# Sums of gated products in the up-projection: half products and sums on VectorE with accumulating DMAs, in place of sums on GpSimd

## The chip, the cores and the metric

The kernel runs on one core of a Trainium2 chip. The metric is the device time of one execution in microseconds (us). The core has five engines that work side by side, each through its own instructions in order: TensorE (PE, matmuls; PEld is its weight load), VectorE (DVE), ScalarE (ACT), GpSimd (POOL) and SyncE (SP, which here only issues DMAs). They meet through semaphores. DMAs move data between DRAM and the on-chip memory; the kernel issues them from SP's queue, from ScalarE's and, after the change, from GpSimd's.

## The reference

One layer of a causal encoder on `x` of shape [1, 2048, 1024]: a gated linear attention mixer, and then a feed-forward block with a causal depthwise convolution. The change lies in the second:

```python
def conv_ffn(h, w_up, conv_w, conv_b, w_down):
    u = causal_dwconv(h @ w_up, conv_w, conv_b)      # h: 2048 x 1024, u: 2048 x 5632
    g, val = jnp.split(u, 2, axis=-1)
    return (jax.nn.silu(g) * val) @ w_down           # (2048 x 2816) @ (2816 x 1024)
```

`causal_dwconv` adds, for each channel, three neighbouring tokens with a weight each and a bias. All is float32.

## The kernel before

The large matrix products are done by Strassen's method in Winograd's form: both operands are cut in 2 x 2 blocks, and seven products `p1` to `p7` of sums of blocks replace eight. float32 accuracy comes from splitting each operand into a high and a low part (`split`, L188 a cast on ScalarE, L189 a subtraction on VectorE) and multiplying three times (`mm3p`, L179 to L181).

The program runs in stages. The mixer takes the first 873 us or so. Then comes the up-projection (`phase_u`), in two halves of 1024 tokens (`s` = 0 and 1; 877 to 1357 us and 1357 to 1750 us of the profile), and then the down-projection (to the end).

In the up-projection the 22 blocks of 128 features are taken in pairs, `f` = 2g and 2g + 1, 11 groups in each half. For a group, the order of jobs is p1, p5, p6, p7, p4, p2, p3, each for the even and then the odd feature, 12 matmuls of 128x512 per job. `ua` and `uc` are PSUM banks that several products add to; what must be kept of `ua` on the way is copied out by ScalarE as `c` (L1237 after p1 and p6; L1333 after p7) before the next product adds to it. The finished columns `u` (both the gate's and the value's) go through the convolution (`conv`: L1253 ACT, L1255 twice DVE, L1257 ACT for silu) into `t`, 128 features by 1024 tokens.

`gated(s, f)`, called at the end of p3, multiplies gate and value (L1262). What the down-projection needs are the seven sums of blocks of that product. With a11 and a21 the two halves of the even feature's tokens and a12 and a22 those of the odd feature's, they are p1 = a11, p2 = a12, p4 = a22, p5 = a21 + a22, p6 = p5 - a11, p3 = a12 - p6 and p7 = a11 - a21. `tiles2` gives the two halves of a tile, each four blocks of 128. The first three are stored as they are (SP's DMAs, L1266, L1269, L1270), the other four are made on GpSimd (L1276, L1280, L1278, L1280) in tiles with the tag `as` and stored by SP (L1282), all to `ad[s, o, q]` in DRAM.

The tag `as` has six buffers (`AB`). They are shared: the copies `c` of L1333 use them, and, in the first half only, the operands `h2p` that are prepared for the second half (`spread` over `prep_h2`: ScalarE casts the high part, VectorE subtracts for the low part, ScalarE issues the two DMAs to `hd`, L841). A tile can only be filled when the last reader of that buffer is done, DMAs among them. The second half then reads `hd` through SP (L904, `h_p`).

The weights of a group are loaded two jobs and seven jobs into the group before it (`load`, L1204, tiles `ur`, by SP). Sums of weights (`us`, L1214 to L1232) are made on GpSimd.

Functions given to `later_do(us, fn)` are issued when a modelled clock, which `adv` moves by each matmul's modelled time, has gone that far. Within each engine the order of instructions is then set by a scheduler when the program is built, so an edit can move instructions that it doesn't name.

In the down-projection `use` adds the seven products to the output (`xe`, `xd` for two blocks of tokens, `acc` for partial sums, `pb` for the bank). `load_step` (L1388) reads `ad` as `da`, L1464 loads the residual `xs` from `x1d`.

Of the kernel before, what the change touches and what calls it, by code (L numbers as in the profile page):

```python
# [10 lines left out]
F32 = mybir.dt.float32  # L11
# [3 lines left out]
ALU = mybir.AluOpType  # L15

P = 128
# [8 lines left out]
def hybrid_kernel(  # L26
# [17 lines left out]
    nc = tc.nc  # L44
    x = x[0]
# [19 lines left out]
    AB = 6  # L65
# [26 lines left out]
    DLEAD = 4  # L92
    DLOAD = 6
    DWLOAD = 3

    cst = ctx.enter_context(tc.tile_pool(name="cst", bufs=1))
    gx = ExitStack()
# [12 lines left out]
    pools = {}  # L110

    def scratch(shape, name):
        return dr.tile(shape, F32, tag=name, name=name)
# [10 lines left out]
    ad = {(s, o, q): scratch([P, 512], f"ad_{s}_{o}_{q}") for s in range(NS) for o in OPS for q in range(NQ)}  # L124

    def mm_ps(name):
        return ps.tile([P, 512], F32, tag="mm", name=name, bufs=4)
# [23 lines left out]
    def later_do(us, fn):  # L151
        heapq.heappush(delayed, (clock["now"] + us, next(seq), fn))
# [1029 lines left out]
    def tiles2(ap):  # L1182

        v = ap.rearrange("p (j c k) -> p c j k", c=2, k=P)
        return v[:, 0], v[:, 1]

    def tiles1(ap):
        return ap.rearrange("p (j k) -> p j k", k=P)
# [3 lines left out]
    def phase_u():  # L1192
        raws, wops, sums, made = {}, {}, {}, {}
# [46 lines left out]
        def new_u(s, i, f):  # L1240
            c = f + i * NF
            u = pools["us"].tile([P, TS + 2], F32, tag="u", name=f"u_{s}_{c}", bufs=3)
            nc.gpsimd.tensor_copy(u[:, 0:2], halo[:, c, :])
            made["u", i, f] = u
            return tiles2(u[:, 2:2 + TS])
# [13 lines left out]

        def gated(s, f):  # L1260
            t, v = made.pop(("t", 0, f)), made.pop(("t", 1, f))
            nc.vector.tensor_mul(t, t, v)  # L1262
            made["a", f % 2] = tiles2(t)
            q = f // 2
            if f % 2 == 0:
                nc.sync.dma_start(tiles1(ad[s, "p1", q]), made["a", 0][0])  # L1266
                return
            (a11, a21), (a12, a22) = made["a", 0], made["a", 1]
            nc.sync.dma_start(tiles1(ad[s, "p2", q]), a12)  # L1269
            nc.sync.dma_start(tiles1(ad[s, "p4", q]), a22)  # L1270
            last = None
            for o, fn, x, y in (("p5", "add", a21, a22), ("p6", "sub", None, a11), ("p3", "rsub", None, a12), ("p7", "sub", a11, a21)):
                t = pools["us"].tile([P, 512], F32, tag="as", name=f"as_{s}_{q}_{o}", bufs=AB)
                tv = tiles1(t)
                if fn == "add":
                    nc.gpsimd.tensor_add(tv, x, y)  # L1276
                elif fn == "rsub":
                    nc.gpsimd.tensor_sub(tv, y, last)  # L1278
                else:
                    nc.gpsimd.tensor_sub(tv, last if x is None else x, y)  # L1280
                last = tv
                nc.sync.dma_start(ad[s, o, q], t)  # L1282

        load(0, 0)
        load(0, 1)
# [3 lines left out]
        for k, (s, g, o, f) in enumerate(jobs):  # L1289
# [23 lines left out]
            if o == "p1":  # L1313
                a = bank["a", f] = mm_ps(f"ua_{s}_{f}")
# [5 lines left out]
            elif o == "p6":  # L1320
                a = bank["a", f]
                mm3p(a, pairs, first=False, more=True)
                made["u2", f] = copied(f"c2_{s}_{f}", a)
            elif o == "p2":
                pb = mm_ps(f"ub_{s}_{f}")
                mm3p(pb, pairs)
                ev, _ = new_u(s, 0, f)
                nc.vector.tensor_add(ev, tiles1(pb), tiles1(made.pop(("p1", f))))  # L1328
            elif o == "p7":
                a = bank["a", f]  # L1330
                mm3p(a, pairs, first=False, more=True)
                u3 = pools["us"].tile([P, 512], F32, tag="as", name=f"c3_{s}_{f}", bufs=AB)
                nc.scalar.copy(u3, a)  # L1333
                ev, od = new_u(s, 1, f)
                made["ev", f] = ev
                nc.vector.tensor_add(od, tiles1(bank["c", f]), tiles1(u3))
            elif o == "p4":
                a = bank.pop(("a", f))
                mm3p(a, pairs, first=False, more=True)
                nc.scalar.copy(made.pop(("ev", f)), tiles1(a))  # L1340
                conv(s, 1, f)
            else:
                c = bank.pop(("c", f))
                mm3p(c, pairs, first=False, more=True)
                _, od = tiles2(made["u", 0, f][:, 2:2 + TS])
                nc.vector.tensor_add(od, tiles1(c), tiles1(made.pop(("u2", f))))
                conv(s, 0, f)
                gated(s, f)
# [4 lines left out]
    araw, wraw, aops, wops, chain, xs, acc, wgrp = {}, {}, {}, {}, {}, {}, {}, {}  # L1353
# [20 lines left out]
    def load_wr(k):  # L1374
        o, s, q = steps[k]
        if s == 0:
            wraw[o, q] = []
            for ij in blocks_of(o):
                r = next(dstep["wr"])
                nc.sync.dma_start(r, block(q, *ij))  # L1380
                wraw[o, q].append(r)
# [35 lines left out]
    def d_load(n):  # L1417
        while dstep["wloaded"] < min(len(steps), n - DLOAD + DWLOAD):
            load_wr(dstep["wloaded"])
            dstep["wloaded"] += 1  # L1420
        while dstep["loaded"] < min(len(steps), n):
            load_step(dstep["loaded"])
            dstep["loaded"] += 1
# [42 lines left out]
    def final_tile(t, nw):  # L1466
        n = 2 if t + 2 == S // P else 1
        sls = [slice(i * D // n, (i + 1) * D // n) for i in range(n)]
        x = xs[t]
        junk = acc[t // TT, t % TT // 2].bitcast(BF16)  # L1470
        ssq = small("ssq", f"ssqf_{t}", 2, "f")
        for i, sl in enumerate(sls):
            nc.scalar.activation(junk[:, sl], x[:, sl], AF.Square, accum_out=ssq[:, i:i + 1])
        var = small("var", f"varf_{t}", 1, "f")
        if n == 2:
            nc.vector.tensor_add(ssq[:, 0:1], ssq[:, 0:1], ssq[:, 1:2])
        nc.vector.tensor_scalar(var, ssq[:, 0:1], 1.0 / D, EPS, op0=ALU.mult, op1=ALU.add)
        rstd = small("rstd", f"rstdf_{t}", 1, "f")
        nc.gpsimd.tensor_tensor(rstd, var, neghalf, op=ALU.pow)
        for sl in sls:  # L1480
            nc.vector.scalar_tensor_tensor(x[:, sl], x[:, sl], rstd, nw[:, sl], op0=ALU.mult, op1=ALU.mult)
            nc.scalar.dma_start(out[t * P:(t + 1) * P, sl], x[:, sl])

    def use(o, s, m, pb, nw):

        e, d = s * TT + 2 * m, s * TT + 2 * m + 1
        c1, c2 = slice(0, 512), slice(512, 1024)
        xe, xd = xs[e], xs[d]
        add = nc.vector.tensor_add
        if o == "p1":  # L1490
            acc[s, m] = dx.tile([P, 512], F32, tag=f"acc{s}_{m}", name=f"acc_{s}_{m}")
            nc.scalar.copy(acc[s, m], pb)
            add(xe[:, c1], xe[:, c1], pb)
        elif o == "p5":
            add(xd[:, c2], xd[:, c2], pb)
            add(xe[:, c2], xe[:, c2], pb)
        elif o == "p6":
            add(acc[s, m], acc[s, m], pb)
            nc.gpsimd.tensor_add(xe[:, c2], xe[:, c2], acc[s, m])
        elif o == "p7":  # L1500
            add(acc[s, m], acc[s, m], pb)
            nc.gpsimd.tensor_add(xd[:, c1], xd[:, c1], acc[s, m])
            nc.gpsimd.tensor_add(xd[:, c2], xd[:, c2], acc[s, m])
        elif o == "p2":
            add(xe[:, c1], xe[:, c1], pb)
        elif o == "p4":
            add(xd[:, c1], xd[:, c1], pb)
            final_tile(d, nw)
        else:
            add(xe[:, c2], xe[:, c2], pb)  # L1510
            final_tile(e, nw)

    nwf = dx.tile([P, D], F32, tag="nwf", name="nwf")
    more = [dx.tile([P, 512], F32, tag=f"wr{i}", name=f"dwr_{i}") for i in range(2 * (DWLOAD + 1) - len(dstep["wr"]))]
    dstep["wr"] = itertools.cycle(dstep["wr"] + more)
    for n, (o, s) in enumerate(units):
        banks = [(mm_ps if n % 2 == 0 else aux_ps)(f"pd_{o}_{s}_{m}") for m in range(PAIRS)]
        last = n + 1 == len(units)
# [53 lines left out]
```

## Time and profile before

| | |
|---|---|
| three runs | 2180.76, 2174.13, 2181.27 us; median 2180.76 |
| profiled execution | span 2176.4 us from the first to the last instruction; its own device time isn't listed apart from the three runs |
| instructions | 28914 |
| mean granted TensorE clock | 0.986 |
| TensorE's longest waits outside the change's stages | 11.7 us for `x` (L383) at the start, 6.1 us for `og` (L728) in five places |
| DMA traffic | 411.76 MB, mean 189 GB/s |
| DMA queues | hardware queues only: q1 48.2%, q10 8.6% of 16 engines' span |

Each row of a view of the profile reads: start and duration in us, engine, line of the kernel, operation, `out<-in` by the program's names, shapes, and in brackets the idle time before it and what ended it. A name ending in `_p` stands for several tiles of a kind. `SPq` and `ACTq` are the issuing of DMAs on SP and ScalarE. In grouped rows, busy time and mean ns of one stand behind the count, then the idle time before them with its most frequent cause.

### The profile page before, as it was taken

To read this page: it belongs to the slowest core of one execution; us is meant where nothing else is said; L and a number is where in the kernel's file an instruction comes from. 1 tells how busy PE (TensorE), PEld (TensorE's weight loads), DVE (VectorE), ACT (ScalarE), POOL (GpSimd) and SP (SyncE) were. 2 spreads that over 40 slices of the span, in tenths; PEclk is the share of its full clock that TensorE was granted. 3 is DMA by queue.
4 is the path that set the end of the run, shared out by engine and by line. 5 is a ranking of instruction groups with operands and counts; after the bars stand their busy time and mean duration, and the time that the engine had idled before them with its cause. 6 is when DMAs were issued, how large, how long until landed. Compare 5 with 4: busy or idle time off the path is not lost.

```text
span 2176.4 us, 28914 instructions
## 1 busy us (share of the span) xinstructions
PE 2086.0 (96%) x9832; PEld 1730.6 (80%) x9832; DVE 1648.3 (76%) x2168; ACT 1104.3 (51%) x2024; POOL 734.9 (34%) x606
## 2 busy tenths in 40 slices
PE   7999999989998999799999998999999999999998
PEld 5788788878887887677888777888888877888886
DVE  8756888798888663778899776988888776457564
ACT  5555756665565775444554453554445533333342
POOL 2000011111111002456666554666565444037010
PEclk9999999999999999999999999999999999999999
DMA  6646684578557999654453458242424567254453
GB/s 219 223 165 211 213 297 137 159 229 298 178 195 251 323 344 365 207 163 131 146 184 102 146 177 291 88 131 76 139 77 124 187 247 269 97 184 160 141 182 113
DMA packets 305124, 411.76 MB, mean 189 GB/s; under 512 B 23742, under 2 KB 160110, under 8 KB 304976
## 3 DMA queue, kind: packets, MB, share of 16 engines
q1 hardware_dynamic: 267440, 346.99, 48.2%
q10 hardware_dynamic: 37536, 62.93, 8.6%
q8 instruction: 77, 1.26, 0.2%
q14 instruction: 71, 0.58, 0.1%
HBM read 266.70 MB, written 143.13 MB: 188 GB/s over the span
## 4 chain that ended last, share of the span: by engine, by line
PE 65%; DVE 13%; DMA 10%; issue 6%; ACT 2%; POOL 2%; SPq 0%; ACTq 0%; DVEq 0%; POOLq 0%
PE pd_p L180 5%; PE pd_p L181 5%; PE pd_p L179 5%; PE ua L179 5%; PE ua L180 5%; PE ua L181 5%; DVE t L1255 4%; DMA h_p<-hd_p 2%; PE uc L179 2%; PE uc L181 2%; PE uc L180 2%; PE mp_Y L180 2%; PE mp_Y L181 2%; PE mp_Y L179 2%; PE mp_R L179 2%
## 5 line engine op out<-in xcount | busy, mean ns | idle before, releaser
L179 PE MATMUL ua<-h_p,uw_p 128*128 128x512 f32 x704 | 279.0, 396 | 28.0 <-ACT c L1237 23.2
L1255 DVE SCALAR_TENSOR_TENSOR t<-u,cw,t 128x1024 f32<-128x1024 f32 x176 | 270.4, 1542 | 10.3 <-ACT t L1253 9.1
L180 PE MATMUL ua<-h_p,uw_p 128*128 128x512 f32 x704 | 277.7, 394 | 0.0
L181 PE MATMUL ua<-h_p,uw_p 128*128 128x512 f32 x704 | 277.2, 394 | 0.0
L180 PE MATMUL pd_p<-dw_p,da 128*128 128x512 f32 x616 | 240.7, 391 | 3.4 <-DVE da L189 3.4
L181 PE MATMUL pd_p<-dw_p,da 128*128 128x512 f32 x616 | 240.3, 390 | 0.0
L179 PE MATMUL pd_p<-dw_p,da 128*128 128x512 f32 x616 | 240.1, 390 | 0.0
L189 DVE TENSOR_TENSOR da<-da_p,da 128x512 fp32r<-128x512 f32 x154 | 131.4, 906 | 105.4 <-ACT da L188 105.3
L189 DVE TENSOR_TENSOR uw_p<-ur,uw_p 128x512 fp32r<-128x512 f32 x176 | 168.6, 979 | 48.8 <-ACT uw_p L188 48.4
L188 ACT CAST da<-da_p 128x512 fp32r<-128x512 f32 x154 | 85.3, 619 | 207.9 <-PE pd_p L181 149.9
L179 PEld LDWEIGHTS ua<-h_p,uw_p 128*128 128x128 f32 x704 | 134.4, 191 | 59.6 <-ACT c L1237 31.8
L188 ACT CAST uw_p<-us 128x512 fp32r<-128x512 f32 x132 | 82.1, 622 | 169.0 <-POOL us L1217 130.7
L189 DVE TENSOR_TENSOR uw_p<-us,uw_p 128x512 fp32r<-128x512 f32 x132 | 127.9, 978 | 47.8 <-ACT uw_p L188 46.8
L181 PEld LDWEIGHTS ua<-h_p,uw_p 128*128 128x128 f32 x704 | 134.5, 191 | 28.6
L180 PEld LDWEIGHTS ua<-h_p,uw_p 128*128 128x128 f32 x704 | 134.5, 191 | 27.9
L180 PEld LDWEIGHTS pd_p<-dw_p,da 128*128 128x128 f32 x616 | 116.0, 188 | 28.7 <-DVE da L189 4.7
L179 PE MATMUL uc<-h_p,uw_p 128*128 128x512 f32 x352 | 137.2, 390 | 0.9 <-DVE u L1328 0.9
L679 POOL TENSOR_TENSOR r<-r,gnw 128x512 f32<-128x512 f32 x32 | 46.9, 1466 | 268.6 <-ACT r L678 228.2
L181 PE MATMUL uc<-h_p,uw_p 128*128 128x512 f32 x352 | 136.9, 389 | 0.0
L180 PE MATMUL uc<-h_p,uw_p 128*128 128x512 f32 x352 | 136.9, 389 | 0.0
L181 PEld LDWEIGHTS pd_p<-dw_p,da 128*128 128x128 f32 x616 | 116.1, 188 | 24.1
L179 PEld LDWEIGHTS pd_p<-dw_p,da 128*128 128x128 f32 x616 | 116.1, 188 | 24.0
(278 smaller groups left out, 5474.8 us busy)
## 6 DMA issues: line engine op xcount, KB each, us to landing
ur<-in_ffn_w_up_dram SPq DMA_DIRECT2D x168, 256.0 KB, 3.7
da_p<-ad_p SPq DMA_DIRECT2D x154, 256.0 KB, 3.8
h_p<-hd_p SPq DMA_DIRECT2D x56, 512.0 KB, 8.0
ad_p<-as_p SPq DMA_DIRECT2D x88, 256.0 KB, 2.3
ad_p<-t SPq DMA_DIRECT2D x66, 256.0 KB, 3.1
x<-in_x_dram SPq DMA_DIRECT2D x32, 512.0 KB, 4.7
ch<-in_ffn_w_down_dram SPq DMA_DIRECT2D x61, 256.0 KB, 4.2
hr_A_p<-h1d_p SPq DMA_DIRECT2D x56, 256.0 KB, 3.0
```

Of the source, the lines that this page charges most:

```text
L179: nc.tensor.matmul(ps_ap, ah, bl, start=(first and i == 0), stop=False, **kw)
L180: nc.tensor.matmul(ps_ap, al, bh, start=False, stop=False, **kw)
L181: nc.tensor.matmul(ps_ap, ah, bh, start=False, stop=(last and i == len(pairs) - 1), **kw)
L188: nc.scalar.copy(hi, src)
L189: nc.vector.tensor_sub(lo, src, f32(hi))
L679: nc.gpsimd.tensor_mul(r, r, sp["gnw"])
L1255: nc.vector.scalar_tensor_tensor(t, u[:, k:k + TS], cw[:, k, c:c + 1], t, op0=ALU.mult, op1=ALU.add)
```

## The change

`gated` makes the two halves of each product apart, and the sums differently. For each feature, VectorE multiplies the second half into a tile `odd` of tag `as`, the first half in place, and adds both into `both`, a second tile of tag `as`. SP stores the first half (p1 or p2) at once. For the even feature it also stores `odd` as p5, and `both` as p6, p3 and p7; for the odd feature it stores `odd` as p4. Then three DMAs on GpSimd's queue add the odd feature's tiles to what lies in DRAM: `odd` to p5 and to p6, `both` to p3. They are issued 6 modelled us later (`TACC`).

So p5 = a21 + a22, p6 = a11 + a21 + a22, p3 = a11 + a21 + a12 + a22, p7 = a11 + a21: the signs of the odd blocks are turned within the method, and three additions in `use` become subtractions for that. The number of plain stores is seven per pair in both, with five for the even feature and two for the odd one now, against one and six. The 88 sums on GpSimd are gone; VectorE has 88 products of 512 columns and 44 sums in place of 44 products of 1024; 66 accumulating DMAs of 256 KB are new. Six tiles `as` were not all filled for a pair before (four were); it is four now, too (two for each feature).

```diff
+    TACC = 6.0
...
         def gated(s, f):
             t, v = made.pop(("t", 0, f)), made.pop(("t", 1, f))
-            nc.vector.tensor_mul(t, t, v)
-            made["a", f % 2] = tiles2(t)
             q = f // 2
+            odd, both = (pools["us"].tile([P, 512], F32, tag="as", name=f"as{n}_{s}_{f}", bufs=AB) for n in "ob")
+            (te, to), (ve, vo) = tiles2(t), tiles2(v)
+            nc.vector.tensor_mul(tiles1(odd), to, vo)
+            nc.vector.tensor_mul(te, te, ve)
+            nc.vector.tensor_add(tiles1(both), te, tiles1(odd))
+            nc.sync.dma_start(tiles1(ad[s, ("p1", "p2")[f % 2], q]), te)
             if f % 2 == 0:
-                nc.sync.dma_start(tiles1(ad[s, "p1", q]), made["a", 0][0])
+                for o, src in (("p5", odd), ("p6", both), ("p3", both), ("p7", both)):
+                    nc.sync.dma_start(ad[s, o, q], src)
                 return
-            (a11, a21), (a12, a22) = made["a", 0], made["a", 1]
-            nc.sync.dma_start(tiles1(ad[s, "p2", q]), a12)
-            nc.sync.dma_start(tiles1(ad[s, "p4", q]), a22)
-            last = None
-            for o, fn, x, y in (("p5", "add", a21, a22), ("p6", "sub", None, a11), ("p3", "rsub", None, a12), ("p7", "sub", a11, a21)):
-                t = pools["us"].tile([P, 512], F32, tag="as", name=f"as_{s}_{q}_{o}", bufs=AB)
...
-                nc.sync.dma_start(ad[s, o, q], t)
+            nc.sync.dma_start(ad[s, "p4", q], odd)
+            for o, src in (("p5", odd), ("p6", odd), ("p3", both)):
+                later_do(TACC, lambda o=o, src=src: nc.gpsimd.dma_start(ad[s, o, q], src, accum_op=ALU.add))
...
         elif o == "p5":
             add(xd[:, c2], xd[:, c2], pb)
-            add(xe[:, c2], xe[:, c2], pb)
+            sub(xe[:, c2], xe[:, c2], pb)
         elif o == "p6":
-            add(acc[s, m], acc[s, m], pb)
+            sub(acc[s, m], acc[s, m], pb)
...
         elif o == "p7":
             add(acc[s, m], acc[s, m], pb)
-            nc.gpsimd.tensor_add(xd[:, c1], xd[:, c1], acc[s, m])
-            nc.gpsimd.tensor_add(xd[:, c2], xd[:, c2], acc[s, m])
+            nc.gpsimd.tensor_sub(xd[:, c1], xd[:, c1], acc[s, m])
+            nc.gpsimd.tensor_sub(xd[:, c2], xd[:, c2], acc[s, m])
```

How the instructions stand on three engines, as the built program has them (line, operation, output and inputs with the tiles' numbers, shape). First VectorE at the end of the third group of the first half (features 4 and 5; `t_4` and `t_5` are their gates, `t_26` and `t_27` their values, `uw` the splits of weights). Before:

```order
L1255 SCALAR_TENSOR_TENSOR t_4_10514<-u_4_10471,cw,t_4_10514 128x1024
L189 TENSOR_TENSOR uw_6_p_10587<-ur_6_0_10279,uw_6_p_10587 128x512
L1255 SCALAR_TENSOR_TENSOR t_5_10540<-u_5_10492,cw,t_5_10540 128x1024
L1262 TENSOR_TENSOR t_4_10514<-t_4_10514,t_26_10423 128x1024
L1255 SCALAR_TENSOR_TENSOR t_5_10540<-u_5_10492,cw,t_5_10540 128x1024
L189 TENSOR_TENSOR uw_7_p_10616<-ur_7_0_10282,uw_7_p_10616 128x512
L189 TENSOR_TENSOR uw_6_p_10634<-ur_6_1_10380,uw_6_p_10634 128x512
L1262 TENSOR_TENSOR t_5_10540<-t_5_10540,t_27_10449 128x1024
L189 TENSOR_TENSOR uw_7_p_10650<-ur_7_1_10383,uw_7_p_10650 128x512
L189 TENSOR_TENSOR h2p_p_1_10595<-h2r_0_10572,h2p_p_0_10594 128x512
L189 TENSOR_TENSOR uw_6_p_10667<-ur_6_1_10380,uw_6_p_10667 128x512
```

After (`aso` is `odd`, `asb` is `both`):

```order
L1256 SCALAR_TENSOR_TENSOR t_5_10554<-u_5_10498,cw,t_5_10554 128x1024
L1266 TENSOR_TENSOR aso_4_10525<-t_4_10520,t_26_10429 128x512
L1267 TENSOR_TENSOR t_4_10520<-t_4_10520,t_26_10429 128x4x128
L1256 SCALAR_TENSOR_TENSOR t_5_10554<-u_5_10498,cw,t_5_10554 128x1024
L1268 TENSOR_TENSOR asb_4_10526<-t_4_10520,aso_4_10525 128x512
L190 TENSOR_TENSOR uw_7_p_10622<-ur_7_0_10285,uw_7_p_10622 128x512
L1266 TENSOR_TENSOR aso_5_10559<-t_5_10554,t_27_10455 128x512
L1267 TENSOR_TENSOR t_5_10554<-t_5_10554,t_27_10455 128x4x128
L190 TENSOR_TENSOR uw_6_p_10643<-ur_6_1_10386,uw_6_p_10643 128x512
L1268 TENSOR_TENSOR asb_5_10560<-t_5_10554,aso_5_10559 128x512
L190 TENSOR_TENSOR uw_7_p_10659<-ur_7_1_10389,uw_7_p_10659 128x512
L190 TENSOR_TENSOR h2p_p_1_10601<-h2r_0_10578,h2p_p_0_10600 128x512
```

Between the product of feature 4 and the low part `h2p_p_1` stood five instructions; there are ten between the first half product and that low part now.

Then SP at the end of the first half (features 20 and 21; `ad_p` are the stores, `h_p` the operands of the second half). Before:

```order
L1266 DMA ad_p_10_352<-t_20_13138 512x1x128
L1269 DMA ad_p_10_407<-t_21_13164 512x1x128
L1270 DMA ad_p_10_396<-t_21_13164 512x1x128
L1282 DMA ad_p_10_363<-as_10_p_13172 128x512
L1282 DMA ad_p_10_374<-as_10_p_13175 128x512
L1282 DMA ad_p_10_418<-as_10_p_13178 128x512
L1282 DMA ad_p_10_385<-as_10_p_13181 128x512
L904 DMA h_p_13184<-hd_p_0_334 128x2x512
```

After:

```order
L1269 DMA ad_p_10_352<-t_20_13168 512x1x128
L1272 DMA ad_p_10_363<-aso_20_13173 128x512
L1272 DMA ad_p_10_374<-asb_20_13174 128x512
L1272 DMA ad_p_10_418<-asb_20_13174 128x512
L1272 DMA ad_p_10_385<-asb_20_13174 128x512
L1269 DMA ad_p_10_407<-t_21_13202 512x1x128
L1274 DMA ad_p_10_396<-aso_21_13207 128x512
L905 DMA h_p_13214<-hd_p_0_334 128x2x512
```

Four stores that came last, behind GpSimd's sums, now stand with the even feature, and none of the seven reads a tile that GpSimd fills.

Last, GpSimd at the end of the first group (features 0 and 1). Before:

```order
L1243 COPY u_2_10144<-halo 128x2
L1276 TENSOR_TENSOR as_0_p_9897<-t_0_9861,t_1_9889 128x512
L1280 TENSOR_TENSOR as_0_p_9900<-as_0_p_9897,t_0_9861 128x512
L1278 TENSOR_TENSOR as_0_p_9903<-t_1_9889,as_0_p_9900 128x512
L1280 TENSOR_TENSOR as_0_p_9906<-t_0_9861 128x512
L1214 TENSOR_TENSOR us_4_10147<-ur_4_0_9948,ur_4_1_10053 128x512
```

After:

```order
L1244 COPY u_2_10147<-halo 128x2
L1276 DMA ad_p_0_353<-aso_1_9902 128x512
L1276 DMA ad_p_0_364<-aso_1_9902 128x512
L1276 DMA ad_p_0_408<-asb_1_9903 128x512
L1215 TENSOR_TENSOR us_4_10150<-ur_4_0_9948,ur_4_1_10056 128x512
```

The three accumulating DMAs stand where the four sums stood, ahead of the next group's sums of weights.

More of the change, by code (lines that the diff above doesn't have):

```diff
@@ L1261, in gated @@
             t, v = made.pop(("t", 0, f)), made.pop(("t", 1, f))
-            nc.vector.tensor_mul(t, t, v)
-            made["a", f % 2] = tiles2(t)
             q = f // 2
+            odd, both = (pools["us"].tile([P, 512], F32, tag="as", name=f"as{n}_{s}_{f}", bufs=AB) for n in "ob")
[4 more added lines that the diff above has]
+            nc.sync.dma_start(tiles1(ad[s, ("p1", "p2")[f % 2], q]), te)
             if f % 2 == 0:
-                nc.sync.dma_start(tiles1(ad[s, "p1", q]), made["a", 0][0])
+                for o, src in (("p5", odd), ("p6", both), ("p3", both), ("p7", both)):
+                    nc.sync.dma_start(ad[s, o, q], src)
                 return
-            (a11, a21), (a12, a22) = made["a", 0], made["a", 1]
-            nc.sync.dma_start(tiles1(ad[s, "p2", q]), a12)
-            nc.sync.dma_start(tiles1(ad[s, "p4", q]), a22)
-            last = None
-            for o, fn, x, y in (("p5", "add", a21, a22), ("p6", "sub", None, a11), ("p3", "rsub", None, a12), ("p7", "sub", a11, a21)):
-                t = pools["us"].tile([P, 512], F32, tag="as", name=f"as_{s}_{q}_{o}", bufs=AB)
[L1274 to L1282, printed above, removed]
+            nc.sync.dma_start(ad[s, "p4", q], odd)
+            for o, src in (("p5", odd), ("p6", odd), ("p3", both)):
+                later_do(TACC, lambda o=o, src=src: nc.gpsimd.dma_start(ad[s, o, q], src, accum_op=ALU.add))
         load(0, 0)
@@ L1488, in use @@
         xe, xd = xs[e], xs[d]
-        add = nc.vector.tensor_add
+        add, sub = nc.vector.tensor_add, nc.vector.tensor_sub
         if o == "p1":
```

## The prediction

> **What bounds the kernel now.** I read the page's busy line first, then a table of busy times by stage (columns: stretch in us, its length, busy time and count for each engine, granted TensorE clock, DMA share, GB/s).
>
> ```profile
> PE 2086.0 (96%) x9832; PEld 1730.6 (80%) x9832; DVE 1648.3 (76%) x2168; ACT 1104.3 (51%) x2024; POOL 734.9 (34%) x606
> 877.00:1357.00 480.00, 449.98 (x1922) 368.39 (x1922) 395.12 (x389) 231.76 (x352) 274.41 (x221) 0.97 0.53 169
> 1357.00:1750.00 393.00, 393.00 (x1734) 325.55 (x1735) 335.82 (x314) 195.47 (x295) 233.29 (x165) 1.00 0.39 119
> 1750.00:2176.40 426.40, 414.53 (x1818) 341.89 (x1817) 254.08 (x324) 143.71 (x261) 114.87 (x83) 0.99 0.51 175
> ```
>
> TensorE is the bound. The rows are the first half of the up-projection, its second half, and the down-projection. In the second half PE is busy for 393.00 of 393.00 us at a clock of 1.00: nothing that the change takes off VectorE or GpSimd there can be won. Only the first half (30 us idle, clock 0.97) and the start of the down-projection are open. PE's list of waits says for what (us, times, longest):
>
> ```profile
> PE ua L179 <- ACT c L1237: 23.2, 8, 6.6
> PE ub L179 <- DMA h_p<-hd_p: 5.1, 1, 5.1
> PE pd_p L180 <- DVE da L189: 3.4, 3, 2.1
> ```
>
> The eight waits of 23.2 us are one kind. In the first half, at a group's end, p7's matmuls may not add to the bank `ua` before ScalarE has copied it (`c`, L1237), and ScalarE comes late. Here is one, by engine: start, duration, and in brackets the wait before it.
>
> ```profile
> 968.78 0.50 PE L179 MATMUL ua<-h_p,uw_p 128*128 128x512 f32 x1 [3.74 <-ACT c L1237]
> 961.59 2.85 ACTq L841 DMA_DIRECT2D hd_p<-h2p_p  x2
> 967.62 0.62 ACT L188 CAST h2p_p<-h2r 128x512 fp32r<-128x512 f32 x1 [5.55 <-DMA ad_p<-as_p]
> 968.15 0.58 ACT L1237 COPY c<-ua 128x512 f32<-128x512 f32 x1
> 961.86 1.67 POOL L1276 TENSOR_TENSOR as_p<-t,t 128x512 f32<-128x512 f32 x1 [1.19 <-DVE t L1262]
> 963.61 1.62 POOL L1280 TENSOR_TENSOR as_p<-as_p,t 128x512 f32<-128x512 f32 x1
> 965.31 1.59 POOL L1278 TENSOR_TENSOR as_p<-t,as_p 128x512 f32<-128x512 f32 x1
> 966.87 1.26 POOL L1280 TENSOR_TENSOR as_p<-t 128x512 f32<-128x512 f32 x1
> 963.56 4.91 SPq L1282 DMA_DIRECT2D ad_p<-as_p  x4
> 957.02 1.22 DVE L1262 TENSOR_TENSOR t<-t,t 128x1024 f32<-128x1024 f32 x1
> 958.15 1.28 DVE L1255 SCALAR_TENSOR_TENSOR t<-u,cw,t 128x1024 f32<-128x1024 f32 x1
> 959.35 1.28 DVE L189 TENSOR_TENSOR uw_p<-ur,uw_p 128x512 fp32r<-128x512 f32 x2
> 960.56 1.23 DVE L1262 TENSOR_TENSOR t<-t,t 128x1024 f32<-128x1024 f32 x1
> 961.70 0.68 DVE L189 TENSOR_TENSOR uw_p<-ur,uw_p 128x512 fp32r<-128x512 f32 x1
> 962.30 1.78 DVE L189 TENSOR_TENSOR h2p_p<-h2r,h2p_p 128x512 fp32r<-128x512 f32 x1
> 964.00 1.78 DVE L189 TENSOR_TENSOR uw_p<-ur,uw_p 128x512 fp32r<-128x512 f32 x1
> ```
>
> Two things hold ScalarE. Its DMA at 961.59 (2.85 us on its queue) stores a low part that VectorE ends only at 964.08: beside the four sums that 128x512 subtraction took 1.78 us, just before them 0.68. Then the next cast of `h2p_p` wants a slot of `as`, the tag that the sums use, and that slot's sum is still on its way to DRAM: 5.55 us idle. The copy for which PE waits stands behind that cast.
>
> **The clock.** After the longer gaps the granted clock falls. Same columns as above, for stretches behind four gaps:
>
> ```profile
> 924.40:930.00 5.60, 5.60 (x15) 4.45 (x16) 2.64 (x5) 2.33 (x5) 0.65 (x1) 0.57 0.96 310
> 969.00:980.00 11.00, 11.00 (x42) 8.90 (x42) 6.55 (x9) 4.08 (x8) 5.45 (x4) 0.84 0.72 213
> 1211.00:1220.00 9.00, 9.00 (x30) 7.21 (x31) 3.68 (x6) 3.48 (x7) 3.33 (x3) 0.72 0.83 233
> 1348.00:1356.00 8.00, 7.99 (x25) 6.09 (x25) 5.63 (x7) 4.58 (x6) 1.11 (x1) 0.72 1.10 355
> ```
>
> Length times (1 − clock) is 2.4 + 1.8 + 2.5 + 2.2 = 8.9 us lost, which the gaps bring with them.
>
> **The change, part by part.** *GpSimd's sums go*, four per pair of features, 88 in all, about 6 us in a row per pair. They are on no path of their own, so what counts is what they slow or hold.
>
> *VectorE's order.* Each product of 1024 columns becomes two halves, and one sum is added:
>
> ```profile
> L1262 DVE TENSOR_TENSOR t<-t,t 128x1024 f32<-128x1024 f32 x44 | 55.7, 1269 | 0.0
> L1336 DVE TENSOR_TENSOR u<-uc,c 128x512 f32<-128x512 f32 x44 | 30.3, 689 | 38.5 <-ACT c L1333 38.5
> ```
>
> A pair goes from 2 × 1.27 = 2.5 us to 6 × 0.69 = 4.1, so 1.6 us more, 35 us over 22 pairs. Against that VectorE saves about 1.1 us for each of some three or four instructions that now run at 0.68 and not 1.78. Its share in these stages is 82 to 85%, so that neither is felt as load; only order and place count. By the order of the place above, ahead of the late low part stand now, from 957.0 on, six half products and sums (6 × 0.69), the scaled sum (1.28) and three splits of 0.68, then the low part itself at 0.68: it ends at about 964.3, as against 964.08. So the slowed subtraction is repaid by the longer queue: no gain and no loss from ScalarE's first wait. I take 0; the ends are −1 us per group, if the sums' slowing reached further than one row, and +1.4, if the accumulating DMAs slow it as the sums did.
>
> *The slots.* Here is the gain. A slot of an even feature's product is now filled on VectorE by about 960.0 (product at 957.0, two halves, the scaled sum, the sum), and SP writes it out at once, where the sums were filled at 963.5 to 968.1. From the page's row on DMAs (KB, median us to landing)
>
> ```profile
> h_p<-hd_p SPq DMA_DIRECT2D x56, 512.0 KB, 8.0
> ad_p<-as_p SPq DMA_DIRECT2D x88, 256.0 KB, 2.3
> ```
>
> it lands 2.3 us behind its issue; four issues stand in a row, about 1.2 us each as before (4.91 / 4), the last at about 963.2, so the slot is free at 965.5 where the cast now starts at 967.62. The gap of 3.74 becomes about 1.6: 57% goes. At this place the cast waits for such plain writes, not for an accumulating one. I carry that share to all eight: 23.2 becomes 10, **13 us saved**. Ends: 0 and 23.2.
>
> *SP's queue.* SP no longer waits for GpSimd in front of loads. At the end of the first half:
>
> ```profile
> 1332.82 5.42 SPq L1282 DMA_DIRECT2D ad_p<-as_p  x4
> 1338.33 2.56 SPq L904 DMA_DIRECT2D h_p<-hd_p  x4
> ```
>
> The loads behind those writes are the ones PE waits 5.1 us for. In the new order SP's last write for that pair needs only VectorE's half product, and the loads follow 5.4 us sooner. I take **4 us saved**, leaving 1 for the three accumulating DMAs that run beside them. Ends: 0 and 5.1.
>
> *Clock.* Of the gaps behind the four rows, 924 keeps about 2.9 us by the same share, the others 2.1 and less. I keep the 2.4 us of the first and a little more: **6 us saved**. Ends: 0 and 8.9.
>
> *Accumulating DMAs.* 66 new ones on GpSimd's queue, each waiting for VectorE, for the landing of the plain write that it adds to, and nothing like them in this trace. GpSimd has 6 us per pair free for them. Price of one on GpSimd, by the nearest rows: between 0 and a sum's 1.67 us; of its landing, between 2.3 us (256 KB written) and 8.0 (the slowest listed above, 512 KB). I take about 1 and 3, near the write, since the size is the same. Three then end by 963.1 (last sum) + 3 × 1 + 3 = 969. What waits behind them on GpSimd is next needed later:
>
> ```profile
> 974.39 1.79 POOL L1214 TENSOR_TENSOR us<-ur,ur 128x512 f32<-128x512 f32 x1 [6.27 <-DMA hd_p<-h2p_p]
> 976.22 0.59 ACT L1333 COPY c<-ua 128x512 f32<-128x512 f32 x1 [1.99 <-POOL us L1214]
> ```
>
> So they cost nothing here, and that cover is 5 to 7 us wide.
>
> The row pair 0.68 and 1.78 us agrees with the Trainium skill ("SBUF — State Buffer", section "Who interferes with whom"), by which a VectorE instruction with two inputs in SBUF contends with a GpSimd instruction that reads there. The same section infers that the descriptors of a GpSimd DMA do not contend with such an instruction; by that the slot for +1.4 us per group would fall away, and the sum stays as it is. No run so far shows it.
>
> *Sign changes in the down-projection* replace an addition by a subtraction on the same engine and shape: 0.
>
> Sum: 13 + 4 + 6 = 23 us off. Against the span of 2176.4 that is 2153.4. The median of the runs shown is 2180.76, 4.4 us over the span (which of the three was profiled isn't listed; the one of 2174.13 wasn't, being shorter). So 2176.4 + 4.4 − 23 = **2158 us**. What remains late next is the low part on VectorE, about 1 to 2 us at several group ends.
>
> **Rivals.** *A, the gain is hidden.* The low part at 964.3 and the DMA behind it hold ScalarE anyway, and the freed slot is not what ends last in most groups. Then only SP's 4 us and little of the clock come: within 6 us of before, about 2177. For it: the low part is no earlier by my own count. Against it: 5.55 us of waiting at the cast, put down to `ad_p<-as_p`.
>
> *B, a new wait, slower.* Copies `c` (L1333) and casts of `h2p_p` take slots that accumulating DMAs still read. If one lands at 8.0 us and each adds 1.67 us on GpSimd, the last is done at 963.1 + 5.0 + 8.0 = 976.1, against 973 to 976 for the copies, and the casts come earlier. Price: each us past the cover is one us of PE in each of the 10 groups of the first half. The 23 us are gone from 2.3 us past it; at 4 us past, 2180.76 − 23 + 40 = 2198. For it: in the program's order some casts at group ends wait for these DMAs. Against it: the same size written lands in 2.3.
>
> The Trainium skill ("DMA: Bandwidth & Descriptors", section "Anatomy of one DMA — SWDGE (gpsimd) path") gives 2.0 us and the bytes over 436 GB/s: an estimate of 2.6 us for 256 KB, for a plain transfer. With it rival B would not happen.
>
> *C, late loads at the start of the down-projection.*
>
> ```profile
> 1773.46 4.96 SPq L1464 DMA_DIRECT2D xs<-x1d  x8
> ```
>
> The second of these now waits for every accumulating DMA, with GpSimd's other sums between them. If the last three run one after another at 8.0 us from 1763 on, that is 1787 and the loads come 13 us late: 2158 + 13 = 2171.
>
> *D, the whole of it goes:* all gaps and clock losses above vanish, 23.2 + 5.1 + 8.9 + 3.4 = 40.6 off: 2140.
>
> **Chances.** The forecast's own case (2148 to 2167) 0.56, A 0.15, B 0.12, C 0.09, D 0.08. A measurement of this kernel tells about 0.3%, 6.5 us, from no change. Faster: the forecast, C and D, with a little of A, 0.75; same: most of A and a mild B, 0.15; slower: the rest of B, 0.10. The range goes from D's 2140 to a mild B at 2184.
>
> **What would show it.** Right: the eight waits of `ua` on `c` sum to about 10 us and not 23; the wait of `ub` on `h_p` is near 1; the 128x512 subtraction at group ends takes 0.7 and not 1.8; POOL's busy time falls by over 100 us; clock in the first half 0.98 to 0.99; no change in the second half. Wrong: ScalarE or PE waiting for `ad_p` from GpSimd's queue (B), the same 23 us under another releaser (A), VectorE waiting for `xs` longer than 6 us after 1770 (C), or a slower VectorE beside the accumulating DMAs.

## The result and the profile after

The changed kernel takes 2192.61 us in the median of four runs (2190.89 to 2196.06). The kernel before took 2181.02 beside it. The ratio is 1.0066, with a 95% interval from 1.0047 to 1.0085: slower by 0.66%, where 2158 us and a gain of 1% had been forecast. The profiled execution took 2190.89 us, with a span of 2189.2.

Here are the busy line of the page after the change, the same three stretches (columns as before), and PE's waits from 870 us on.

```profile
PE 2084.3 (95%) x9832; PEld 1727.5 (79%) x9832; DVE 1628.7 (74%) x2256; ACT 1105.8 (51%) x2024; POOL 669.2 (31%) x584
877.00:1357.00 480.00, 445.48 (x1911) 363.13 (x1911) 377.37 (x428) 229.28 (x349) 245.27 (x209) 0.98 0.62 181
1357.00:1750.00 393.00, 380.05 (x1666) 313.76 (x1665) 321.70 (x348) 192.25 (x287) 191.89 (x151) 0.99 0.52 138
1750.00:2189.20 439.20, 430.48 (x1899) 356.44 (x1897) 264.06 (x339) 150.10 (x271) 119.87 (x88) 0.99 0.53 177
PE ua L180 <- ACT c L1238: 38.2, 14, 6.0
PE ua L180 <- ACT c L1327: 9.0, 3, 7.8
PE uc L180 <- DVE u L1322: 3.3, 1, 3.3
PE ub L180 <- issue: 1.6, 1, 1.6
```

The eight waits of 23.2 us for `c` stand against 14 waits of 38.2 us. One of the 14 doesn't belong to the group ends: the wait at the very start of the up-projection, which the profile before puts down to `h_p` and this one to the copy `c`. Before, and after:

```profile
PE ua L179 <- DMA h_p<-hd_p: 4.7, 1, 4.7
```

```profile
876.68 0.80 PE L180 MATMUL ua<-h_p,uw_p 128*128 128x512 f32 x1 [4.71 <-ACT c L1238]
```

So what was 23.2 us in eight waits is 33.5 us in 13. A second kind, 9.0 us for the other copy, is new. The second stretch was without a gap (393.00 of 393.00); now PE is busy for 380.05 us of it. Against that, 1.6 of the 5.1 us before `ub` are left, and the 3.4 us for `da` in the down-projection are gone. The DMA share of the second stretch rose from 0.39 to 0.52.

What became of the place that the prediction took apart, the end of the third group:

```profile
960.84 0.69 DVE L190 TENSOR_TENSOR h2p_p<-h2r,h2p_p 128x512 fp32r<-128x512 f32 x1
962.02 0.62 ACT L189 CAST h2p_p<-h2r 128x512 fp32r<-128x512 f32 x1 [2.18 <-DVE h2p_p L190]
963.60 0.58 ACT L1238 COPY c<-ua 128x512 f32<-128x512 f32 x1 [0.96 <-ACT h2p_p L189]
964.23 0.50 PE L180 MATMUL ua<-h_p,uw_p 128*128 128x512 f32 x1 [4.34 <-ACT c L1238]
960.86 0.88 POOL L1276 DMA_DIRECT2D ad_p<-asb  x1
```

The steps of the forecast are there. The low part takes 0.69 us and not 1.78 (the median of the 28 low parts of this stage went from 1.77 to 0.69 us), beside the issue of an accumulating DMA on GpSimd (last row), as the Trainium skill infers ("SBUF — State Buffer", section "Who interferes with whom"). The cast no longer waits 5.55 us for a slot. And yet PE waits 4.34 us, not 1.6. The copy comes 4.6 us earlier than before (963.60 and 968.15), but PE is through with the matmuls ahead of it 5.2 us earlier (959.89 and 965.04, the starts less the waits). What holds the copy here is the low part on VectorE, the wait for which the prediction had set no gain and no loss. The rows on DMAs show what else has changed (queues: packets, MB, share of 16 engines' span; issues: count, KB, median us to landing). Before:

```profile
q1 hardware_dynamic: 267440, 346.99, 48.2%
ur<-in_ffn_w_up_dram SPq DMA_DIRECT2D x168, 256.0 KB, 3.7
hd_p<-h2p_p ACTq DMA_DIRECT2D x56, 256.0 KB, 3.2
```

After:

```profile
q1 hardware_dynamic: 258992, 346.99, 48.2%
q0 software_dynamic: 9504, 17.31, 5.1%
ur<-in_ffn_w_up_dram SPq DMA_DIRECT2D x168, 256.0 KB, 7.5
hd_p<-h2p_p ACTq DMA_DIRECT2D x56, 256.0 KB, 5.5
ad_p<-aso POOLq DMA_DIRECT2D x44, 256.0 KB, 6.5
ad_p<-asb POOLq DMA_DIRECT2D x22, 256.0 KB, 9.0
```

The accumulating DMAs land in 6.5 and 9.0 us, not in 3, and they are not free to others: a weight load `ur` takes 7.5 us, twice as long as before. The new queue moves 17.31 MB, 5% of what q1 moves, and takes 5.1% of the engines' span for it, against 48.2% for twenty times as much. Per byte that is 2.1 times as long.

Who is late is seen at the end of another group. The first sum of weights on GpSimd before the change, and after it:

```profile
1175.55 1.29 POOL L1214 TENSOR_TENSOR us<-ur,ur 128x512 f32<-128x512 f32 x1 [4.33 <-DMA ur<-in_ffn_w_up_dram]
```

```profile
1181.37 1.46 POOL L1215 TENSOR_TENSOR us<-ur,ur 128x512 f32<-128x512 f32 x1 [10.50 <-DMA ur<-in_ffn_w_up_dram]
```

By the timelines GpSimd was done with what came ahead at 1171.2 us before (the last sum) and at 1170.9 after (the last issue), so the sums of weights begin 6 us later on nearly the same clock.

### The profile page after: what moved, and what is told of

The parts are those of the page before. It is cut to its first block, busy times and chain, and to the rows that moved or that the text cites. A ratio compares the mean times of both kernels' runs of the same rounds, so it can differ in the third digit from the quotient of the medians.

```text
span 2189.2 us, 29063 instructions
## 1 busy us (share of the span) xinstructions
PE 2084.3 (95%) x9832; PEld 1727.5 (79%) x9832; DVE 1628.7 (74%) x2256; ACT 1105.8 (51%) x2024; POOL 669.2 (31%) x584
## 3 DMA queue, kind: packets, MB, share of 16 engines
q1 hardware_dynamic: 258992, 346.99, 48.2%
q0 software_dynamic: 9504, 17.31, 5.1%
q8 instruction: 77, 1.26, 0.2%
## 4 chain that ended last, share of the span: by engine, by line
PE 63%; DVE 12%; DMA 10%; issue 7%; POOL 3%; ACT 3%; SPq 1%; ACTq 0%; DVEq 0%; POOLq 0%
PE pd_p L182 6%; PE pd_p L181 6%; PE pd_p L180 6%; PE ua L180 4%; PE ua L181 4%; PE ua L182 4%; DVE t L1256 4%; DMA ur<-in_ffn_w_up_dram 3%; PE mp_R L180 2%; PE uc L182 2%; PE uc L181 2%; PE uc L180 2%; PE mp_R L182 2%; PE mp_R L181 2%; PE mp_Y L182 2%
## 5 line engine op out<-in xcount | busy, mean ns | idle before, releaser
L180 PE MATMUL ua<-h_p,uw_p 128*128 128x512 f32 x704 | 280.9, 399 | 47.2 <-ACT c L1238 38.2
L1256 DVE SCALAR_TENSOR_TENSOR t<-u,cw,t 128x1024 f32<-128x1024 f32 x176 | 287.1, 1636 | 11.5 <-ACT t L1254 10.5
L190 DVE TENSOR_TENSOR uw_p<-ur,uw_p 128x512 fp32r<-128x512 f32 x176 | 125.9, 729 | 59.2 <-ACT uw_p L189 59.0
L1215 POOL TENSOR_TENSOR us<-ur,ur 128x512 f32<-128x512 f32 x44 | 74.4, 1690 | 217.7 <-DMA ur<-in_ffn_w_up_dram 196.8
```

What stands on the lines that cost most here:

```text
L180: nc.tensor.matmul(ps_ap, ah, bl, start=(first and i == 0), stop=False, **kw)
L190: nc.vector.tensor_sub(lo, src, f32(hi))
L1215: add(src, a21, a22)
L1256: nc.vector.scalar_tensor_tensor(t, u[:, k:k + TS], cw[:, k, c:c + 1], t, op0=ALU.mult, op1=ALU.add)
```

## The experiments

Three theories stood at the start. T: the traffic of the accumulating DMAs makes the loads late. O: the plain stores, now earlier and closer together, collide with the loads. V: VectorE's longer queue holds ScalarE. Ratios are to the kernel before, on the same chip, with a 95% interval; since that kernel's median differed between the sets (2176 to 2181 us), ratios are what to compare across them.

**Without the accumulating DMAs.** p5, p6 and p3 lack the odd feature's part.

```diff
-            for o, src in (("p5", odd), ("p6", odd), ("p3", both)):
-                later_do(TACC, lambda o=o, src=src: nc.gpsimd.dma_start(ad[s, o, q], src, accum_op=ALU.add))
```

> The changed kernel without its 66 accumulating DMAs (p5, p6 and p3 then lack the odd feature's part). Theory T: these DMAs keep the DMA engines busy at the end of each group, so that the weight loads `ur` land late (7.5 us in the median with the change, 3.7 before) and everything behind them; then this kernel falls below the one before, to about 2160 us (2150 to 2170), and `ur` lands in about 4 us. Theory O: the plain stores, which now come earlier and close together, are what the loads collide with; theory V: VectorE's ten more instructions ahead of the low part are what holds ScalarE. By O or V it stays at 2185 to 2195.

2151.19 us, ratio 0.9874 (0.9856 to 0.9892). All that the change does besides these DMAs is worth 1.3%, more than the 1.0% forecast for the whole. O and V fall as causes of the loss. (V's ten more instructions were miscounted: the two orders shown ahead of the prediction have nine instructions between the first half product and the low part, not ten, and five before, so four more.) PE's waits from 870 us on, the wait at the start of the up-projection, the one at the end of the third group, and the loads:

```profile
PE ua L180 <- ACT c L1238: 16.3, 8, 4.5
PE uc L180 <- DVE u L1320: 2.6, 1, 2.6
PE ua L180 <- ACT c L1325: 1.2, 1, 1.2
876.33 0.54 PE L180 MATMUL ua<-h_p,uw_p 128*128 128x512 f32 x1 [4.49 <-ACT c L1238]
959.52 0.50 PE L180 MATMUL ua<-h_p,uw_p 128*128 128x512 f32 x1 [2.31 <-ACT c L1238]
ur<-in_ffn_w_up_dram SPq DMA_DIRECT2D x168, 256.0 KB, 4.9
```

The loads land in 4.9 us, not quite in the 3.7 of before: a little of O is there. But of the 16.3 us, 4.49 are the wait at the start, so the group ends cost 11.8 us in seven waits, half of the 23.2 of before.

**As plain stores on GpSimd's queue**, into a scratch of their own:

```diff
-                later_do(TACC, lambda o=o, src=src: nc.gpsimd.dma_start(ad[s, o, q], src, accum_op=ALU.add))
+                later_do(TACC, lambda o=o, src=src: nc.gpsimd.dma_start(ax[s, o, q], src))
```

> The changed kernel with the 66 DMAs on GpSimd's queue as plain stores into a scratch of their own, without the addition (p5, p6 and p3 lack the odd feature's part). If it is the issue on GpSimd's queue and the bytes written that cost, the time stays near the changed kernel's, 2185 to 2193. If it is the read and write back of the addition (whose packets take about twice as long as others in the table of queues), most of the cost goes: 2165 to 2175. Theories O and V: 2185 to 2195.

2171.96 us, ratio 0.9962 (0.9949 to 0.9974). A little over half of the loss goes with the addition (1.04 of 1.92%). The same bytes on the same queue now take half the engines' time (below), and `ur` lands in 6.2 us. Two smaller things go with the addition too: GpSimd's issue takes 0.55 and not 0.9 to 1.0 us, and no DMA has to wait for the plain store that it adds to, for which GpSimd stood idle 6.1 us in three places in the changed kernel. (By the table of queues an accumulating packet had taken 2.9 times as long as one of q1, not twice; 2.1 times is the figure per byte.)

```profile
q0 software_dynamic: 5280, 17.31, 2.6%
ax_p<-aso POOLq DMA_DIRECT2D x44, 256.0 KB, 3.8
ax_p<-asb POOLq DMA_DIRECT2D x22, 256.0 KB, 5.6
```

**The same plain stores on SP's queue:**

```diff
-                later_do(TACC, lambda o=o, src=src: nc.gpsimd.dma_start(ad[s, o, q], src, accum_op=ALU.add))
+                later_do(TACC, lambda o=o, src=src: nc.sync.dma_start(ax[s, o, q], src))
```

> The 66 DMAs as plain stores into a scratch (p5, p6 and p3 lack the odd feature's part), on SP's queue and not on GpSimd's. On GpSimd's queue they gave 2172. If it is the bytes and the held slots that cost the 21 us above 2151: again 2168 to 2176. If it is GpSimd's queue: 2151 to 2160. Should SP's waits for the odd feature hold its loads back: above 2176.

2161.45 us, ratio 0.9933 (0.9918 to 0.9948), between the two cases that had been written down. In ratios, then: plain stores of these bytes, with the tiles that they hold, 0.59% (0.9874 to 0.9933); GpSimd's queue in place of SP's 0.29% more, whose intervals just part; and the addition another 1.04% (to 1.0066).

**The kernel before, with three accumulating DMAs per pair added**, into a scratch that nothing reads:

```diff
                 nc.sync.dma_start(ad[s, o, q], t)
+                if o != "p7":
+                    later_do(6.0, lambda o=o, t=t: nc.gpsimd.dma_start(ax[s, o, q], t, accum_op=ALU.add))
```

> The kernel before, with three accumulating DMAs per pair added, of the same size and as many modelled us later, into a scratch that nothing reads. Theory T: slower than before by 15 to 30 us, 2195 to 2210, with `ur` landing in 6 us or more. Theories O and V: within 5 us of 2181, since its stores and VectorE's work are as before.

2232.28 us, ratio 1.0248 (1.0224 to 1.0271): 2.5% slower, more than T had set. Its largest wait of PE:

```profile
PE ua L180 <- ACT c L1238: 57.6, 13, 7.8
```

So these DMAs cost in a kernel with the old stores and the old order, too, which speaks against O and V once more. But it is not traffic alone that costs here. They come behind or between GpSimd's four sums and hold the sums' tiles longer: by the waits of this profile VectorE and ScalarE stood idle for tiles that these DMAs still read, 57.8 us in 14 places (low parts 31.9, casts of `h2p_p` 20.1, copies `c` 5.8), which is the mechanism of rival B. In the changed kernel those waits are 4.8 us in three places. How the excess divides was not tried.

**From another tile.** This parts traffic from held slots, the mechanism of rival B. The DMAs read one operand that stays in place, so no `as` tile waits for them (the sums get other values).

```diff
+        if o == "p3":
+            hop["raw"] = f32(t[:, 0, 0, :])
...
-nc.gpsimd.dma_start(ad[s, o, q], src, accum_op=ALU.add)
+nc.gpsimd.dma_start(ad[s, o, q], hop["raw"], accum_op=ALU.add)
```

> The changed kernel with its accumulating DMAs reading a tile that stays in place (one operand of the first product group) and not the `as` tiles: the same bytes, queue, destinations and additions (the sums get other values), but no `as` slot is held by them. If what costs 41 us between 2151 (without them) and 2192.6 is that casts and copies wait for slots which these DMAs still read, the time falls to 2155 to 2165. If it is their traffic, which delays `ur` and the stores of `h2p`, it stays at 2180 to 2195, with `ur` landing in 7 us or more.

2192.84 us, ratio 1.0073 (1.0055 to 1.0090): nothing is won by freeing the slots. `ur` stays late:

```profile
ur<-in_ffn_w_up_dram SPq DMA_DIRECT2D x168, 256.0 KB, 7.7
ad_p<-h_p POOLq DMA_DIRECT2D x66, 256.0 KB, 7.3
```

So rival B gave the right sign by the wrong mechanism for this kernel. What is left is the traffic, and the queue of GpSimd that these DMAs stand in. Against the queue speaks that GpSimd stood idle 36.3 us in front of them in the changed kernel and 65.4 us in this run, and the intervals of the two ratios overlap.

**Issued 16 modelled us later** (`TACC = 16.0`).

> The changed kernel with its accumulating DMAs issued 16 and not 6 modelled us after the odd product, past the burst of plain stores and weight loads. If traffic in the burst costs: 2170 to 2185, with `ur` landing in about 5 us. If held slots cost, the slots are held 10 us longer: 2195 to 2215.

2192.87 us, ratio 1.0081 (1.0066 to 1.0096). This decides nothing: in the profile the DMAs stand at the same places on GpSimd, and only a few rows of other work at the very end have moved. Whether the same traffic at a quieter time would cost less stays open.

**One per pair** (p3's alone; p5 and p6 lack the odd feature's part).

> The changed kernel with one accumulating DMA per pair, to p3, instead of three (p5 and p6 lack the odd feature's part). None gave 2151, three 2192.6. If each costs the same, (2192.6 - 2151) / 3 = 13.9 us for 22 of them: 2165 (2160 to 2170). If they cost only where three in a row pile up: below 2158. If the first one already makes the loads late: above 2175.

2162.02 us, ratio 0.9932 (0.9913 to 0.9952). The first 22 cost 0.58%, the other 44 then 1.34%, 0.67% for each 22. The cost grows with their number from the first on.

**In the first half alone** (p5, p6 and p3 of the second half lack the odd feature's part).

> The changed kernel with its accumulating DMAs in the first half of the up-projection alone (p5, p6 and p3 of the second half lack the odd feature's part). By the profiles, of the 41 us between 2151 and 2192.6 some 20 lie in the first half and 22 in the second: 2171 (2166 to 2176). If the second half was only late from what the first left behind: 2185 or more.

2180.00 us, ratio 1.0020 (1.0007 to 1.0033), below the 2185 of the one case and above the other's range. The first half's DMAs cost 1.46% (0.9874 to 1.0020), the second half's 0.46%. The split into 20 and 22 us was misread: it came from stretches cut at fixed times (1357 us), and in the slower kernel the first half is not over by then. By VectorE's first `odd` product (L1266) in the second half, at 1346.86 us without the DMAs, 1377.95 with all of them and 1378.71 here, the first half loses 31 us. From there to the last such product it is 386.9, 395.3 and 386.3 us: 8 us for the second half with them, and none without, so nothing is left over from the first.

**All sums on VectorE, no accumulating DMA.** The kernel before, with its four sums moved:

```diff
-                    nc.gpsimd.tensor_add(tv, x, y)
+                    nc.vector.tensor_add(tv, x, y)
...
-                    nc.gpsimd.tensor_sub(tv, y, last)
+                    nc.vector.tensor_sub(tv, y, last)
...
-                    nc.gpsimd.tensor_sub(tv, last if x is None else x, y)
+                    nc.vector.tensor_sub(tv, last if x is None else x, y)
```

> The kernel before, with its four sums per pair on VectorE in place of GpSimd; no accumulating DMA. Theory T: faster than before, about 2165 (2155 to 2175), since neither GpSimd's sums nor accumulating DMAs are there, at the price of 2.8 us of VectorE per pair, which its idle 15 to 18% covers. Theory V: VectorE's longer queue at the group's end holds ScalarE more than now, 2190 or more.

2164.63 us, ratio 0.9938 (0.9914 to 0.9962): faster than both kernels. Four sums of 0.68 us cost VectorE more than the change's two, and they pay. PE's wait for `c` is still 22.3 us here, 3.16 of it at the start of the up-projection:

```profile
PE ua L179 <- ACT c L1237: 22.3, 10, 5.3
961.72 0.62 ACT L188 CAST h2p_p<-h2r 128x512 fp32r<-128x512 f32 x1 [4.95 <-DMA ad_p<-as_p]
```

In it the cast still waits for a slot that a late sum fills, 4.95 us, for which the change's early stores are the remedy.

**The same spread over both features**, in the signs of the change: p7 at the even one; p6 = p7 + a22, p3 = p6 + a12 and p5 at the odd one.

```diff
+            if f % 2 == 0:
+                nc.sync.dma_start(tiles1(ad[s, "p1", q]), te)
+                made["p7s"] = summed("p7", te, to)
+                return
...
+            p6 = summed("p6", made["p7s"], to)
+            summed("p3", p6, te)
+            summed("p5", made["a", 0][1], to)
```

> All sums on VectorE and no accumulating DMA, in the changed kernel's signs: p7 is made and stored at the even feature, p6 = p7 + a22, p3 = p6 + a12 and p5 at the odd one; whole products of 1024 columns. By traffic, and with VectorE's work spread over both features: at or below the kernel with all four sums at the odd feature (2164.6), 2155 to 2165. If VectorE's load at the group's end is what is left to win, 2158 or less; if its load anywhere counts, about 2165.

2164.54 us, ratio 0.9947 (0.9928 to 0.9965), not to be told from the one before it. Spreading the sums wins nothing that can be measured.

**The same with p7's sum on GpSimd.**

> The kernel with all sums on VectorE spread over both features (2164.5), but p7's sum on GpSimd, one per pair. If the 0.7 us that VectorE saves at each pair is worth more than one GpSimd sum beside it: 2156 to 2162. If one GpSimd sum slows VectorE by the 1.1 us seen beside it: 2164 to 2170.

2178.35 us, ratio 0.9993 (0.9978 to 1.0009): above the 2164 to 2170 of the worse case. One sum on GpSimd per pair takes back nearly all of the gain. Why so much was not settled.

## Why the prediction was wrong

**The bound** was named rightly: PE's waits for `c` in the first half, the clock behind them. But that the second half was without a gap was read only one way, as "nothing to win". It also meant that nothing there had been late enough to show. PE lost 13 us of that stretch, in three gaps: 3.31 us at 1362.63, at the turn of the halves (0.94 us before, just ahead of the stretch), 1.88 us at 1419.19 and 7.75 us at 1745.48. The largest, its cause on ScalarE:

```profile
1744.33 0.62 ACT L189 CAST da<-da_p 128x512 fp32r<-128x512 f32 x1 [10.89 <-DMA da_p<-ad_p]
1744.85 0.58 ACT L1327 COPY c<-ua 128x512 f32<-128x512 f32 x1
1745.48 0.79 PE L180 MATMUL ua<-h_p,uw_p 128*128 128x512 f32 x1 [7.75 <-ACT c L1327]
```

The copy stands behind a cast that waits 10.89 us for a load. Without the accumulating DMAs the cast waits 4.31 us at the same place:

```profile
1704.92 0.62 ACT L189 CAST da<-da_p 128x512 fp32r<-128x512 f32 x1 [4.31 <-DMA da_p<-ad_p]
1705.44 0.58 ACT L1325 COPY c<-ua 128x512 f32<-128x512 f32 x1
```

**The slots, SP's queue and the clock** (13 + 4 + 6 = 23 us): right in kind, and a little too small. The run without the accumulating DMAs shows them by themselves: the same edit is then worth 1.26%, about 27 us. In its profile the waits for `c` at group ends fall from 23.2 to 11.8 us, where 10 had been forecast. The 5.1 us for `h_p` go, where 4 had been taken. PE's busy time falls from 2086.0 to 2075.3 us for the same 9832 matmuls, 10.7 us, where 6 had been taken for the clock (0.97 to 0.99 in the first half). The 3.4 us for `da`, which only rival D had counted, go too.

**VectorE's order** was put at 0. At the third group's end, from the first `odd` product to the end of the low part, the profile after has 7.3 us (954.22 to 961.53), as the prediction had (957.0 to 964.3). Its terms as printed add up to 8.1 us; the rows shorten that, since neighbours of 0.69 us start some 0.6 us apart.

**The accumulating DMAs: here it failed.** "I take about 1 and 3, near the write, since the size is the same", and then "So they cost nothing here". About 1 us for the issue was right (0.88 us in the row above). The landing took 6.5 and 9.0 us, and the upper end that had been set was 8.0. The graver fault is that a DMA was priced only by what waits for it: the engine that issues it and the tile that it reads. What it takes from other transfers was put at nothing, and the price was there even when no `as` tile was held (2192.84 us). The trace had shown the DMA engines at 0.53 in the first half, with bursts above that behind the gaps (0.72 to 1.10 in the four rows on the clock). From 956 to 970 us, where three of these DMAs now fall, the share was 0.78 before and is 1.03 after. No rival was that. The cost term is 0 in the prediction and 1.92% (0.9874 to 1.0066), about 42 us, by the runs.

The estimate of 2.6 us that the prediction worked out from the Trainium skill ("DMA: Bandwidth & Descriptors", section "Anatomy of one DMA — SWDGE (gpsimd) path") rests on a fit that has no term for an addition; the plain ones on that queue took 3.8 and 5.6 us here, the accumulating ones 6.5 and 9.0.

**The chain from late loads to PE** is seen in the profiles and was not cut by an experiment of its own. ScalarE's casts of weights wait for GpSimd's first sum, by the rows of its waits (us, times, longest), first without the accumulating DMAs, then with them; and the convolution on VectorE, the same 176 instructions, is slower with them, as it is beside a GpSimd sum elsewhere (in the profile after, 2.42 us at 948.28 us beside a sum, 1.27 us at 951.23 without one):

```profile
ACT uw_p L189 <- POOL us L1215: 13.7, 5, 5.6
L1256 DVE SCALAR_TENSOR_TENSOR t<-u,cw,t 128x1024 f32<-128x1024 f32 x176 | 256.8, 1464 | 11.5 <-ACT t L1254 10.4
```

```profile
ACT uw_p L189 <- POOL us L1215: 51.5, 23, 10.5
L1256 DVE SCALAR_TENSOR_TENSOR t<-u,cw,t 128x1024 f32<-128x1024 f32 x176 | 287.1, 1636 | 11.5 <-ACT t L1254 10.5
```

That is 38 us more of ScalarE waiting and 30 us more of VectorE's time, in the engines that make PE late. That the sums of weights, shifted by late loads, now fall on the convolution is the reading that fits both rows; it was argued, not shown. Nor can late weight loads be the whole price: `ur` landed in 4.9 us both without the added DMAs and with the plain stores on SP's queue, which cost 0.59%, and in 6.3 us with one accumulating DMA per pair (0.9932) as against 6.2 with three plain stores on GpSimd's queue (0.9962).

**The rest.** POOL's busy time fell by 66 us and not by over 100, because the issues of the DMAs count there (44 of 0.88 us in the median and 22 of 1.04). Rival C, late `xs` loads, did not come: VectorE's waits for `xs` fell from 11.1 to 5.5 us. Rival A, the hidden gain, is refuted by the run without the DMAs.

## What to carry to other kernels

A DMA that is added is to be priced as traffic first: what share of the DMA engines it takes, what else is in flight at that moment, and who waits for those transfers. Moving sums into accumulating DMAs was no saving in this kernel, where the loads for the next step are issued at the same moment; whether a quieter moment would be cheaper was not shown. The plain sums on VectorE, 2.8 us per pair on an engine that was 82 to 85% busy, beat both GpSimd's sums and the DMAs by 0.6% and 1.3%. And a stage without a single wait has nothing to win, but it may have much to lose: look at how late its loads may come.

## What the runs showed of the hardware

An accumulating DMA of 256 KB took twice the engines' time of a plain one on the same queue (5.1% against 2.6% of the span for 17.31 MB). With 66 of them the weight loads of 256 KB on another queue landed in a median of 7.5 us, without them in 4.9. GpSimd took 0.88 to 1.04 us (medians) to issue one and 0.55 a plain one, and a subtraction on VectorE beside that issue ran at its full speed, 0.69 us, where beside a sum on GpSimd it took 1.78.
